# Odd mixer of a two-layer hybrid model: the first projection loaded as one block, smaller temporaries, and the mLSTM query and key products issued five chunks behind the convolution

## The chip, the core and the metric

The kernel runs on one core of one Trainium2 chip. The core has a matrix engine (TensorE, PE in the profile, with its weight loads as PEld), a vector engine (DVE), a scalar engine (ACT) and GpSimd (POOL), each with a queue of its own; SP issues most of the transfers from memory. The metric is the device time of one execution in microseconds; lower is better. Every time is that of the same inputs on the same kind of chip.

## The reference

The model has two layers on 256 rows of width 1024, all in float32. Each layer adds half a SwiGLU feed-forward block, then a mixer, then half of a second feed-forward block; the first layer's mixer is the even one (retention and gated linear attention), the second layer's the odd one (an RG-LRU and an mLSTM). The part that the change is about:

```python
def odd_mixer(hn, ...):
    ly, lx, mu, mv, mo, mi, mf = split_cols(hn @ w_in, ODD_SPLITS)
    lxc = causal_dwconv(f32(lx), f32(lru_conv_w), lru_conv_b)
    lru = rg_lru(lxc, ...)
    lru = lru * jax.nn.gelu(f32(ly))
    mc = jax.nn.silu(causal_dwconv(f32(mu), f32(ml_conv_w), ml_conv_b)).reshape(B, S, ML_HEADS, ML_DH)
    q = jnp.einsum('bshi,hij->bshj', mc, f32(ml_wq))
    k = jnp.einsum('bshi,hij->bshj', mc, f32(ml_wk)) * (ML_DH ** -0.5)
    hm = mlstm(q, k, f32(mv).reshape(B, S, ML_HEADS, ML_DH), f32(mi) + f32(ml_bi), f32(mf) + f32(ml_bf))
    hm = jax.nn.sigmoid(f32(mo)).reshape(B, S, ML_HEADS, ML_DH) * hm
    hm = head_rms(hm).reshape(B, S, -1) * f32(ml_norm_w)
    o = jnp.concatenate([lru, hm], axis=-1)
    return o.astype(hn.dtype) @ w_out
```

`hn @ w_in` is one product of 256 x 1024 with 1024 x 2568; `mi` and `mf` are the 8 gate columns at its end. The mLSTM weighs the products of q and k with a matrix E of exponentials that is made from the gates alone.

## The kernel before

**Precision and splits.** A float32 product is made of three faster ones. Each operand is split in two: `hi` is written by ACT (`split`, line 136) and `lo`, the rest, by DVE (line 137). `mm3` (line 215) then issues hi·hi (line 219), lo·hi (line 220) and hi·lo (line 222) for one block of 128 of the inner dimension; I call the three products of one block a chunk. Small products inside the mixers are plain float32.

**Rows.** The 256 rows are two halves of 128, t = 0 and t = 1. I write lx(0) for the unit lx with the first half. A normalized half stands transposed as `Th` (high) and `Tl` (low), made by `norm` (line 305): eight transposes on PE (line 318), eight `Th` on ACT (line 250), eight `Tl` on DVE (line 251).

**Units.** The program is a list of units, each with a `load` and a `run(t, w)`. The driver at the end of the kernel runs each unit for t = 0 as it comes, and for t = 1 some 1.5 units later (`LAG`). Around the odd mixer this gives the following order: the last blocks b8, b9, b10 of the feed-forward block's down projection (products into `acc`), then the mixer's six projections. mu0 makes 256 columns of mu and the 8 gate columns, mu1 the other 256 of mu, lx 512, mv 512, mo 512, ly 512. On PE this reads b10(0), b8(1), mu0(0), b9(1), mu1(0), b10(1), lx(0), mu0(1), mu1(1), mv(0), lx(1), mo(0) and so on. Four units of the output projection follow, and then the next feed-forward block.

**Rings.** `load_group` (line 139) takes a place in the ring `raw` (three places), has SP fill it, takes a place each in `hi` and `lo` (five places), and issues the splits. A place in `raw` is free again when its block is split, one in `hi` and `lo` when t = 1 has multiplied with it. A place is as large as the largest block of its ring: 2048 columns of float32 before. `proj_unit` (line 797) cuts a projection of n columns into groups of `g` blocks of the inner dimension: all 8 in one group for n up to 256, two groups of 4 above that. mu0 has n = 264 and so takes two groups of 4 x 264 = 1056 columns; mu1 takes one of 8 x 256 = 2048; lx, mv, mo and ly take two groups of 4 x 512 = 2048 each, which I call lx-a, lx-b, mv-a and so on. mu0's groups are split in steps of 2n = 528 columns, the others' in steps of 1024.

**Chains.** Work that hangs on a projection is a generator (`chain`, line 196), which yields a number of chunks after which its next part is issued (`STEPS`). `tick` counts the chunks that `mm3` has issued, those of 256 columns as half. `ml_chain` (line 1307) transposes mu, convolves it on DVE (twelve steps on line 1232), takes the silu by a tanh (line 1313 on ACT, line 1314 on DVE, which gives `mc`), yields `STEPS[18]`, then issues the query and key products (lines 1320 and 1321). `gate_chain` (line 1255) makes E from the gates with rows that are spread to all partitions through memory by POOL (`spread`). `lru_chain` does the same kind of work for lx.

**Order on an engine.** Each engine's instructions are put in order when the program is built: by the order in which they were issued, but with those that the builder expects to be ready placed ahead of those that it expects to wait. `issue_after` ties single ones.

**Temporaries.** Tiles of a mixer come from a pool; `mt(tag, shape, bufs)` says how many places a tag has. Places in question: `E3` and `gst` in the even mixer (lines 940 and 994), and in the odd mixer `mx` and `mrow` (lines 1273 and 1278) and `kw` (line 1336, the keys weighted with E, read on line 1353), and the results of `rsqrt_mean` (line 257). `mW` is the tag of a spread row (line 1287) that t = 1 needs.

Of the kernel before, what the change touches and what calls it, by code (L numbers as in the profile page):

```python
# [11 lines left out]
F32 = mybir.dt.float32  # L12
# [4 lines left out]
ALU = mybir.AluOpType  # L17
AX = mybir.AxisListType

P = 128  # L20
D = 1024
DFF = 2816
KC = D // P
# [23 lines left out]
TRP = 10  # L47
NT = 2
NTF = 10
STEPS = (2, 2, 10, 8, 3, 3, 6, 7, 3, 1, 1, 30, 10, 10, 9, 8, 3, 2, 10, 3, 3, 2, 9, 2, 3)  # L50

SUMS = (8, 4, 4)

# [15 lines left out]
def hybrid_kernel(ctx: ExitStack, tc: tile.TileContext, I, out):  # L69
    nc = tc.nc  # L70
    V, S, T, G = nc.vector, nc.scalar, nc.tensor, nc.gpsimd
# [3 lines left out]
    apool = ctx.enter_context(tc.tile_pool(name="act", bufs=1))  # L75
# [8 lines left out]
    def nm(s):  # L84
        cnt[0] += 1
        return f"{s}_{cnt[0]}"
# [4 lines left out]
    def mt(tag, shape, bufs=1, dt=F32):  # L91
        return pools[-1].tile(list(shape), dt, tag=tag, bufs=bufs, name=nm(tag))
# [161 lines left out]

    def rsqrt_mean(ss, n, w, name):
        m = apool.tile([P, w], F32, tag=f"rm{w}", bufs=2, name=nm("rm"))
        r = apool.tile([P, w], F32, tag=name, bufs=4, name=nm("rs"))
        G.tensor_scalar(out=m, in0=ss, scalar1=1.0 / n, scalar2=EPS, op0=ALU.mult, op1=ALU.add)
        G.tensor_tensor(out=r, in0=m, in1=mh4[:, :w], op=ALU.pow)
        return r  # L260
# [536 lines left out]
    def proj_unit(w_in, cols, body, mixer):  # L797

        wv = w_in.rearrange("(k p) n -> p k n", p=P)
        n = sum(w for _, w in cols)  # L800
        g = KC if n <= 256 else 4

        def load():
            return [load_group([wv[:, k0:k0 + g, c:c + w] for c, w in cols], g, n,
                               step=MSTEP[mixer] if n in (256, 512) else 2 * n) for k0 in range(0, KC, g)]

        def run(t, w):
            xT = get_x(t)
            ps = ps_tile()
            for k in range(KC):  # L810
                hi, lo = w[k // g]
                mm3([(ps[:, :n], slice(0, n))], xT, k, (hi[:, k % g, :], lo[:, k % g, :]), k == 0, k == KC - 1)
            body(t, ps[:, :n], state["rs"][t])
        return load, run, 0.5 if n < 300 else 1
# [57 lines left out]
    def even_units(w_in, w_lr_up, b_lr, w_out, nxt):  # L872
# [37 lines left out]
        def gla_chain(t, gl):  # L910
            d = st[t]
            yield STEPS[0]
            pt = ps_tile(tag="acc")
            T.transpose(pt[:16, :P], gl, ident)
            glT = mt("glTh", [16, P], 1, F32R), mt("glTl", [16, P], 1, F32R)
            split(pt[:16, :P], *glT)
            yield STEPS[1]
            pz = ps_tile(tag="acc")
# [6 lines left out]
            split(la, *lhl)  # L925
            yield STEPS[2]

# [9 lines left out]
                         start=True, stop=True)  # L937
            E1 = mt("E1", [P, 256])
            E2 = mt("E2", [P, 256])
            E3 = mt("E3", [P, 256], 2)  # L940
            E4 = mt("E4", [P, 256])
            dec = mt("dec", [P, 4], 2)
            S.activation(E1, pb[:, 256:], AF.Exp)
# [10 lines left out]
            V.scalar_tensor_tensor(out=E3, in0=k, scalar=0.125, in1=E3, op0=ALU.mult, op1=ALU.mult)  # L954
            yield STEPS[3]
            p1 = ps_tile(tag="acc")
# [14 lines left out]
            for p in range(2):  # L971
                for hh in range(2):
                    r = slice(hh * 64, hh * 64 + 64)
# [11 lines left out]
            for c in range(2 if t == 0 else 1):  # L985
                pu = ps_tile(tag="acc")
                r = slice(c * 64, c * 64 + 64)
# [3 lines left out]
                             v[r, hd, :], start=True, stop=True)  # L991
                upd.append(pu)
            for c, pu in enumerate(upd):
                sn = mt("gst", [P, 2, P], 3)
                if Sst[c] is None:
                    V.tensor_copy(f2(sn), pu[:, :256])
                else:
                    for p in range(2):
                        V.scalar_tensor_tensor(out=sn[:, p, :], in0=Sst[c][:, p, :],
                                               scalar=dec[:, 2 * p + c:2 * p + c + 1],  # L1000
                                               in1=pu[:, p * P:(p + 1) * P], op0=ALU.mult, op1=ALU.add)
                Sst[c + 1] = sn
# [14 lines left out]
            for p in range(2):  # L1017
                for hh, c in ((0, 0), (1, 1), (0, 1), (1, 0)):
                    if Sst[c] is None:
                        continue  # L1020
                    r, cc = slice(hh * 64, hh * 64 + 64), slice(c * 64, c * 64 + 64)
# [138 lines left out]
    def odd_units(w_in, prm, w_out, nxt):  # L1160
# [94 lines left out]
        def gate_chain(t, g8):  # L1255
            d = st[t]
            lf = mt("lf", [P, 4])
            logsigmoid(lf, g8[:, 4:8], "f", 4)
            yield STEPS[14]
            pb = ps_tile(tag="acc")  # L1260
            T.matmul(pb[:, 0:4], C["tri"], lf, start=True, stop=True)
            ab = mt("ab", [P, 2, 4], 2)
            V.tensor_copy(ab[:, 1, :], pb[:, 0:4])
            V.tensor_tensor(out=ab[:, 0, :], in0=g8[:, 0:4], in1=ab[:, 1, :], op=ALU.subtract)
            yield STEPS[15]
            pr = ps_tile(tag="acc")
            T.transpose(pr[:4, 0:P], ab[:, 0, :], ident)
            T.transpose(pr[:4, P:2 * P], ab[:, 1, :], ident)
            arow = mt("arow", [4, 2 * P])
            S.copy(arow, pr[:4, 0:2 * P])  # L1270
            if t == 1:
                yield lambda: "m1" in C
            mx = mt("mx", [4, P], 2)
            V.tensor_tensor_scan(out=mx, data0=arow[:, 0:P], data1=arow[:, 0:P],
                                 initial=0.0 if t == 0 else C["m1"], op0=ALU.max, op1=ALU.max)
            rows = {}
            spread(rows, "E", mx, "mE", 3)
            mrow = mt("mrow", [4, P])
            V.tensor_tensor(out=mrow, in0=arow[:, P:2 * P], in1=mx, op=ALU.add)
            if t == 0:  # L1280
                m1 = mt("m1", [4, 1])
                V.tensor_copy(m1, mrow[:, P - 1:P])
                C["m1"] = m1
            else:
                wi = mt("wi", [4, P])
                S.activation(wi, mx, AF.Exp, scale=-1.0, bias=C["m1"])
                spread(d, "wi", wi, "mW", 3)
            yield STEPS[16]
            pq = ps_tile(tag="acc")
            T.transpose(pq[:, 0:4], mrow, ident[:4, :4])  # L1290
            guard = mt("guard", [P, 4], 2)
            S.activation(guard, pq[:, 0:4], AF.Exp, scale=-1.0)
            yield lambda: "E" in rows
            yield STEPS[24]
            E = rows["E"]
            for hd in range(4):
                V.scalar_tensor_tensor(out=E[:, hd, :], in0=E[:, hd, :], scalar=ab[:, 0, hd:hd + 1],
                                       in1=C["big"], op0=ALU.subtract, op1=ALU.max)
            S.activation(f2(E), f2(E), AF.Exp, scale=-1.0)
            d["E"], d["guard"] = E, guard  # L1300
# [6 lines left out]
        def ml_chain(t, u):  # L1307
# [25 lines left out]
            V.tensor_tensor(out=f2(Sw), in0=psS, in1=f2(E), op=ALU.mult)  # L1333
            if t == 0:
                pk2 = transposes(f2(kT), 4)
                kw = mt("mkw", [P, 4, P])
                for hd in range(4):
                    V.tensor_scalar(out=kw[:, hd, :], in0=pk2[:, hd * P:(hd + 1) * P], scalar1=E[:, hd, P - 1:P],
                                    scalar2=None, op0=ALU.mult)
            else:  # L1340

                yield has(t, "wi")
                V.tensor_tensor(out=f2(qT), in0=f2(qT), in1=f2(d["wi"]), op=ALU.mult)
# [18 lines left out]
            for p in range(2):  # L1362
                pn = ps_tile(tag="acc")
                last = None
                for i in range(2):
                    hd = 2 * p + i
                    sl = slice(i * (P + 1), (i + 1) * (P + 1))
                    with after(last):
                        last = T.matmul(pn[:, sl], Sw[:, hd, :], v[:, hd, :], start=True, stop=t == 0)
                        if t == 1:  # L1370
# [8 lines left out]
                                in1=den[:, hs].unsqueeze(2).to_broadcast([P, 2, P]), op=ALU.mult)  # L1379
# [225 lines left out]
```

## Time and profile before

| | us |
|---|---|
| median of 3 runs | 953.7 |
| lowest and highest run | 952.96, 953.75 |
| the profiled execution | 954.01 |
| its span, first to last instruction | 952.2 |
| PE busy in the span | 941.4 |
| DVE busy | 826.4 |
| ACT busy | 616.1 |
| weight loads busy (PEld) | 777.2 |

A row of the timeline gives the start in microseconds, the length, the engine, the line of the kernel, the operation, what is written and what is read, the shape, and how many equal instructions were merged; in square brackets stands the idle time of the engine just before and what ended it. A number after `x` in a group is the count of instructions, and the next the mean or the range of their durations in ns. Ends of PE's products are modelled: the records of two products that follow each other overlap, so PE's speed is read from the distance of starts. The odd mixer's projections and chains run from about 660 to 760 us.

### The profile page before, as it was taken

What the parts mean: (1) busy time and instruction counts of PE and PEld (TensorE: products, weight loads), DVE (VectorE), ACT (ScalarE), POOL (GpSimd) and SP (SyncE); (2) the same over time, 40 slices, a digit from 0 to 9 for tenths busy, and PEclk for the clock granted to TensorE, in tenths of its full rate; (3) what the DMA queues carried; (4) which work ended last, traced back from release to release, by engine and by line L of the source; (5) the groups of instructions that cost most, each with busy time, mean ns of one, the idle gap of its engine ahead of it and who ended that gap; (6) DMA issues with size and microseconds to landing.
All of it is one profiled execution on the core that took longest, in us unless ns stands there. A gap on an engine that the chain in (4) does not pass through costs nothing.

```text
span 952.2 us, 11885 instructions
## 1 busy us (share of the span) xinstructions
PE 941.4 (99%) x4526; PEld 777.2 (82%) x4526; DVE 826.4 (87%) x970; ACT 616.1 (65%) x815; POOL 22.6 (2%) x49
## 2 busy tenths in 40 slices
PE   9999999999999999999999999999999999999997
PEld 6888888888888888888888888888888788888876
DVE  6999999687776999998489999955797999999996
ACT  7647567584656665765476656654899767566564
POOL 1000000000100000000000000000101000000000
PEclk9999999999999999999999999999999999999999
DMA  9876463755358555649461935474452782944521
GB/s 304 281 279 209 146 221 98 220 172 198 100 185 281 208 183 215 237 138 334 145 229 45 322 108 188 143 229 154 136 183 72 252 321 68 329 151 160 177 89 66
DMA packets 103529, 180.32 MB, mean 189 GB/s; under 512 B 8277, under 2 KB 51441, under 8 KB 103473
## 3 DMA queue, kind: packets, MB, share of 16 engines
q1 hardware_dynamic: 102704, 178.23, 55.5%
q0 software_dynamic: 336, 0.79, 0.3%
q8 instruction: 35, 0.57, 0.2%
q10 hardware_dynamic: 432, 0.55, 0.2%
q14 instruction: 22, 0.17, 0.1%
HBM read 178.50 MB, written 1.05 MB: 189 GB/s over the span
## 4 chain that ended last, share of the span: by engine, by line
PE 84%; DVE 10%; issue 2%; ACT 2%; DMA 1%; POOL 0%; POOLq 0%; ACTq 0%; DVEq 0%
PE ps L653 21%; PE ps L219 11%; PE ps L220 11%; PE ps L222 11%; PE acc L220 8%; PE acc L219 8%; PE acc L222 8%; DVE lo L137 5%; DVE draw L670 2%; PE ps L680 1%; ACT hi L136 1%; PE ps L236 1%; DMA h<-in_x_dram 0%; DVE cs L670 0%; DMA draw<-in_ffn_wgu_dram 0%
## 5 line engine op out<-in xcount | busy, mean ns | idle before, releaser
L137 DVE TENSOR_TENSOR lo<-raw,hi 128x512 fp32r<-128x512 f32 (+4 forms) x211 | 289.9, 1398 | 41.5 <-ACT hi L136 41.4
L136 ACT ACTIVATE hi<-raw 128x512 fp32r<-128x512 f32 (+4 forms) x211 | 244.2, 1197 | 50.6 <-PE ps L222 21.8
L219 PE MATMUL ps<-hi,Th 128*128 128x512 f32 (+3 forms) x512 | 199.2, 389 | 0.3 <-ACT Th L250 0.2
L220 PE MATMUL ps<-lo,Th 128*128 128x512 f32 (+3 forms) x512 | 193.8, 379 | 1.0 <-DVE lo L137 1.0
L222 PE MATMUL ps<-hi,Tl 128*128 128x512 f32 (+3 forms) x512 | 193.8, 379 | 0.0
L137 DVE TENSOR_TENSOR lo<-draw,hi 128x2048 fp32r<-128x2048 f32 (+1 forms) x86 | 182.4, 2138 | 10.0 <-ACT hi L136 10.0
L136 ACT ACTIVATE hi<-draw 128x2048 fp32r<-128x2048 f32 (+1 forms) x86 | 153.8, 1799 | 50.5 <-DVE draw L670 38.1
L219 PE MATMUL acc<-hi,aT 128*128 128x512 f32 x350 | 137.7, 396 | 1.2 <-ACT hi L136 1.2
L220 PE MATMUL acc<-lo,aT 128*128 128x512 f32 x350 | 135.8, 390 | 0.0
L220 PEld LDWEIGHTS ps<-lo,Th 128*128 128x128 f32 x512 | 96.5, 188 | 18.4 <-DVE lo L137 2.4
L219 PEld LDWEIGHTS ps<-hi,Th 128*128 128x128 f32 x512 | 96.2, 188 | 18.0 <-issue 0.7
L222 PE MATMUL acc<-hi,aT 128*128 128x512 f32 x350 | 110.8, 390 | 0.0
L222 PEld LDWEIGHTS ps<-hi,Tl 128*128 128x128 f32 x512 | 96.2, 188 | 17.8 <-DVE Tl L137 0.2
L670 DVE TENSOR_TENSOR draw<-draw,draw 128x2048 f32<-128x2048 f32 x39 | 89.1, 2287 | 2.8 <-DVE lo L137 1.8
L136 ACT ACTIVATE aT<-ps 128x256 fp32r<-128x256 f32 x88 | 33.3, 379 | 77.2 <-PE ps L236 43.9
L219 PEld LDWEIGHTS acc<-hi,aT 128*128 128x128 f32 x350 | 65.7, 188 | 14.7 <-ACT hi L136 1.6
L222 PEld LDWEIGHTS acc<-hi,aT 128*128 128x128 f32 x350 | 65.7, 188 | 13.9
L220 PEld LDWEIGHTS acc<-lo,aT 128*128 128x128 f32 x350 | 65.6, 188 | 12.8 <-DVE lo L137 0.2
L653 PE MATMUL ps<-hi,Th 128*128 128x512 f32 x156 | 61.2, 392 | 0.0
L653 PE MATMUL ps<-hi,Tl 128*128 128x512 f32 x156 | 60.8, 390 | 0.0
L653 PE MATMUL ps<-lo,Th 128*128 128x512 f32 x156 | 60.8, 389 | 0.0
L137 DVE TENSOR_TENSOR aT<-ps,aT 128x256 fp32r<-128x256 f32 x88 | 36.9, 421 | 11.7 <-ACT aT L136 11.3
(379 smaller groups left out, 1279.0 us busy)
## 6 DMA issues: line engine op xcount, KB each, us to landing
raw<-in_ffn_wd_dram SPq DMA_DIRECT2D x44, 1024.0 KB, 5.3
draw<-in_ffn_wgu_dram SPq DMA_DIRECT2D x39, 1024.0 KB, 6.6
raw<-in_ffn_wgu_dram SPq DMA_DIRECT2D x64, 512.0 KB, 5.0
raw<-in_ffn_wgu_dram SPq DMA_DIRECT2D x13, 1024.0 KB, 6.3
raw<-in_e_w_in_dram SPq DMA_DIRECT2D x13, 1024.0 KB, 5.1
raw<-in_o_w_in_dram SPq DMA_DIRECT2D x9, 1024.0 KB, 5.2
raw<-in_e_w_out_dram SPq DMA_DIRECT2D x4, 1024.0 KB, 4.9
raw<-in_o_w_out_dram SPq DMA_DIRECT2D x4, 1024.0 KB, 4.9
```

The costliest lines, as they stand in the source:

```text
L136: S.activation(hi2, src2, AF.Copy)
L137: V.tensor_tensor(out=lo2, in0=src2, in1=hi2.bitcast(F32), op=ALU.subtract)
L219: T.matmul(ps, xh[:, k, :], wk[0][:, sl], start=start, stop=False)
L220: T.matmul(ps, xh[:, k, :], wk[1][:, sl], start=False, stop=False)
L222: state["mm"] = T.matmul(ps, xl[:, k, :], wk[0][:, sl], start=False, stop=stop)
L236: T.transpose(pt[:, i * P:(i + 1) * P], src[:, i * P:(i + 1) * P], ident)
L653: state["mm"] = T.matmul(ps, x[a][:, k, :], w[b][:, k, :], start=first and k == 0 and i == 0, stop=k == 3 and i == 2, skip_group_check=not ...
L670: state["dve"] = V.tensor_tensor(out=out, in0=a, in1=b, op=op)
L680: T.transpose(pt[:, i * P:(i + 1) * P], a[:, i * P:(i + 1) * P], ident)
```

## The change

1. `proj_unit` puts all 8 blocks into one group for n up to 264, so that mu0 becomes one load of 8 x 264 = 2112 columns in place of two of 1056. Its split keeps steps of 528 columns. The places of all three rings, thirteen in all, grow from 2048 to 2112 columns, 256 bytes per partition each.
2. Temporaries get fewer places: `E3` one instead of two, `gst` two instead of three, `mx` one instead of two, the four-wide results of `rsqrt_mean` two instead of four; `mrow` is computed in place in the second half of `arow`; `kw` shares the one place of `mW`.
3. `STEPS[18]` is 5 instead of 10: the query and key products are issued five chunks after the convolution.

```diff
-STEPS = (2, 2, 10, 8, 3, 3, 6, 7, 3, 1, 1, 30, 10, 10, 9, 8, 3, 2, 10, 3, 3, 2, 9, 2, 3)
+STEPS = (2, 2, 10, 8, 3, 3, 6, 7, 3, 1, 1, 30, 10, 10, 9, 8, 3, 2, 5, 3, 3, 2, 9, 2, 3)
...
-        r = apool.tile([P, w], F32, tag=name, bufs=4, name=nm("rs"))
+        r = apool.tile([P, w], F32, tag=name, bufs=4 if w == 1 else 2, name=nm("rs"))
...
-        g = KC if n <= 256 else 4
+        g = KC if n <= 264 else 4
...
-            E3 = mt("E3", [P, 256], 2)
+            E3 = mt("E3", [P, 256])
...
-                sn = mt("gst", [P, 2, P], 3)
+                sn = mt("gst", [P, 2, P], 2)
...
-            mx = mt("mx", [4, P], 2)
+            mx = mt("mx", [4, P])
...
-            mrow = mt("mrow", [4, P])
-            V.tensor_tensor(out=mrow, in0=arow[:, P:2 * P], in1=mx, op=ALU.add)
+            mrow = arow[:, P:2 * P]
+            V.tensor_tensor(out=mrow, in0=mrow, in1=mx, op=ALU.add)
...
-                kw = mt("mkw", [P, 4, P])
+                kw = mt("mW", [P, 4, P], 1)
```

## The prediction, made before the changed kernel was timed

> **What bounds the kernel now.** I read the page first, then the busy times by stretch, the waits of PE in the odd mixer, and the timeline around the longest of them.
>
> ```profile
> span 952.2 us, 11885 instructions
> ...
> PE 941.4 (99%) x4526; PEld 777.2 (82%) x4526; DVE 826.4 (87%) x970; ACT 616.1 (65%) x815; POOL 22.6 (2%) x49
> ```
>
> ```profile
> 660.00:674.50 14.50, 14.50 (x94) 12.89 (x93) 8.64 (x20) 10.91 (x20) 2.03 (x3) 1.00 0.24 76
> 674.50:683.00 8.50, 7.34 (x37) 5.72 (x36) 8.40 (x21) 7.41 (x15) 0.00 (x0) 1.00 0.43 127
> ...
> 692.50:722.00 29.50, 29.09 (x169) 24.29 (x169) 28.28 (x79) 26.61 (x48) 2.29 (x5) 1.00 0.45 152
> ...
> 940.00:952.20 12.20, 6.03 (x33) 5.05 (x31) 7.10 (x18) 4.84 (x17) 0.00 (x0) 0.87 0.26 93
> ```
>
> The columns of the second view are the stretch, its length, the busy time of PE, PEld, DVE, ACT and POOL, the granted clock and the DMA. PE is idle for 952.2 − 941.4 = 10.8 us in all, of which 6.2 lie in the last stretch, behind the last product. No edit here removes a product, so a gain can only be PE time that is lost to waits. In the mixer the largest such place is 674.5 to 683.0: PE is idle for 1.16 us, and DVE is busy for 8.40 of 8.50 us. For those 8.5 us DVE is the bound. In the 14.5 us before it DVE works only 8.64.
>
> ```profile
> PE ps L220 <- DVE lo L137: 1.0, 1, 1.0
> ```
>
> This is the longest of PE's waits from 625 to 760 us. A PE record is longer than its issue distance, so a wait is partly hidden in it; I measure by the distance of starts instead.
>
> ```profile
> 662.52 0.28 PE L219 MATMUL ps<-hi,Th 128*128 128x264 f32 x1
> ...
> 665.30 0.28 PE L222 MATMUL ps<-hi,Tl 128*128 128x264 f32 x1
> ...
> 668.19 0.28 PE L219 MATMUL ps<-hi,Th 128*128 128x256 f32 x1
> ...
> 674.50 0.39 PE L219 MATMUL ps<-hi,Th 128*128 128x512 f32 x1
> 674.73 0.39 PE L220 MATMUL ps<-lo,Th 128*128 128x512 f32 x1
> ...
> 677.43 0.39 PE L219 MATMUL ps<-hi,Th 128*128 128x512 f32 x1
> ...
> 678.46 0.27 PE L1268 MATMUL acc<-ident,ab 128*4 128x128 f32 x1
> 678.93 0.39 PE L219 MATMUL ps<-hi,Th 128*128 128x264 f32 x1 [0.19 <-ACT Th L250]
> 679.15 0.28 PE L220 MATMUL ps<-lo,Th 128*128 128x264 f32 x1
> 680.40 0.50 PE L220 MATMUL ps<-lo,Th 128*128 128x512 f32 x1 [0.96 <-DVE lo L137]
> 680.74 0.40 PE L222 MATMUL ps<-hi,Tl 128*128 128x512 f32 x1
> ...
> 683.03 0.38 PE L1320 MATMUL acc<-mc,wqk 128*128 128x128 f32 x2
> ```
>
> lx(0), the unit lx for the first 128 rows, starts at 674.50. Products of 512 columns start 0.23 us apart; the 24 of mu0(0), 264 columns each, start from 662.52 to 665.30, 2.78 / 23 = 0.12 apart. From 679.15 to 680.74 there are 1.59 us where a 264 and a 512 need 0.12 + 0.23 = 0.35: 1.24 lost. From 678.46 to 679.15 there are 0.69 where a transpose and a 264 after it need at most 0.34 as an estimate (0.12 for each and 0.10 for the change of shape): 0.35 lost. Together **1.6 us**. The product that waits is the second block of lx, of which the low half is not split yet.
>
> ```profile
> 671.20 2.36 DVE L137 TENSOR_TENSOR lo<-raw,hi 128x1024 fp32r<-128x1024 f32 x2 [0.79 <-ACT hi L136]
> ...
> 675.60 3.61 DVE L1232 SCALAR_TENSOR_TENSOR mc<-mlcb,mlcw,mc 128x128 f32<-128x128 f32 x12
> 679.12 2.36 DVE L137 TENSOR_TENSOR lo<-raw,hi 128x1024 fp32r<-128x1024 f32 x2
> 681.39 0.35 DVE L251 SCALAR_TENSOR_TENSOR Tl<-ps,nw,Th 128x128 fp32r<-128x128 f32 x1
> 681.65 0.69 DVE L1314 SCALAR_TENSOR_TENSOR mc<-mE,mc 128x512 f32<-128x512 f32 x1
> ...
> 684.47 0.34 DVE L251 SCALAR_TENSOR_TENSOR Tl<-acc,nw,Th 128x128 fp32r<-128x128 f32 x1
> ```
>
> ```profile
> 661.02 0.37 ACT L250 ACTIVATE Th<-ps,nw 128x128 fp32r<-128x128 f32 x1 [3.00 <-PE ps L318]
> ...
> 676.62 2.00 ACT L136 ACTIVATE hi<-raw 128x1024 fp32r<-128x1024 f32 x2
> ...
> 679.65 1.28 ACT L1313 ACT_TABLE_LOAD   x1
> 680.95 0.64 ACT L1313 ACTIVATE mE<-mc 128x512 f32<-128x512 f32 x1
> ```
>
> The split of that block (ACT 676.62, DVE 679.12) comes behind the twelve steps of the mLSTM convolution on DVE. It could not start before 674.5: hi and lo are rings of five, and five loads ahead of it stands the last block of the FFN's down projection, whose products for the second 128 rows run until lx(0) starts.
>
> **The change part by part.**
>
> *One block for the first projection (term A).* The mixer's loads before are mu0a, mu0b, mu1, lx-a, lx-b, mv-a and so on; after, mu0 is one. Every load from mu1 on takes the ring place that its predecessor had: lx-a waits for the third-last block of the down projection, whose last user ends where mu0(0) begins (662.5), instead of the second-last (668.19, where mu1(0) begins); lx-b for the second-last, instead of the last (674.5). mv-a takes over the wait for the last. So lx-a's split can move to where mu1's stands now, and lx-b's to where lx-a's stands now (ACT about 670, DVE 671.20 to 673.56), over 4 us ahead of its first use, which is after four of lx's chunks and eight transposes. The cover is DVE's 14.50 − 8.64 = 5.9 us of idle time from 660 on; mu1's split moves in front, where ACT idles 3.00 us before 661.02. The same number of products, splits (4 x 528 columns for mu0 in both) and bytes stays; SP issues two transfers instead of four, and nothing waits for SP here. Term A: **−1.6 us**, between 0 and −1.6.
>
> *Query and key products five chunks behind (term D).* They are sixteen fp32 matmul records of the wqk lines, first at 683.03, right behind lx(0): ten chunks after the convolution was issued, two of them in the last down projection, eight in lx(0). Five chunks put them into the order behind lx's third chunk, before 677.43. They need mc, which now comes at 681.65 + 0.69 = 682.3. The convolution ends at 675.60 + 3.61 = 679.2; then tanh (0.64) and L1314 (0.69) make 680.5 where the table load (1.28) lies under the convolution, and 681.8 where it does not. With term A lx(0) ends at 683.03 − 1.6 = 681.4. Whether the built order lets the products wait for mc or fills in others is seen at the second half:
>
> ```profile
> 705.77 0.39 PE L220 MATMUL ps<-lo,Th 128*128 128x512 f32 x1
> 706.15 0.46 PE L1320 MATMUL acc<-mc,wqk 128*128 128x128 f32 x2
> ```
>
> ```profile
> 705.31 0.69 DVE L1314 SCALAR_TENSOR_TENSOR mc<-mE,mc 128x512 f32<-128x512 f32 x1 [0.33 <-ACT mE L1313]
> ```
>
> There the ten chunks are long over (mv(0) and lx(1) were being multiplied), and the products stand in the middle of a chunk at 706.15, where mc was ready at 706.00. The order was made by when operands come, and it was right to 0.15 us (706.15 − 705.77 = 0.38 against 0.23). The wait at 680.40 shows that it can be 1.2 us wrong. Bounds of D: 0 to +1.2; I take **+0.4**, which is 681.8 − 681.4. Earlier products feed nothing that is late: what follows them waits for E, which is made from the gates.
>
> *The smaller temporaries (cost 0).* Each now shares a buffer whose last reader is long done:
>
> ```profile
> 209.23 0.97 PE L990 MATMUL acc<-gv,E 64*64 64x128 f32 x16
> ...
> 214.07 0.65 PE L1023 MATMUL acc<-gst,gqiT 64*64 64x128 f32 x8
> ```
>
> ```profile
> 221.72 0.40 ACT L946 ACTIVATE E<-acc 128x256 f32<-128x256 f32 x1
> ```
>
> ```profile
> 233.94 0.60 DVE L999 SCALAR_TENSOR_TENSOR gst<-gst,dec,acc 128x128 f32<-128x128 f32 x2
> ```
>
> ```profile
> 708.01 1.06 PE L1353 MATMUL acc<-v,mkw 128*128 128x129 f32 x8
> ```
>
> ```profile
> L1251 POOL DMA_DIRECT2D mW<-r x1: 553/553/553, 720.3 to 720.3; - x1
> ```
>
> E3 is read until 210.2 and written again at 221.72; the first gst is read until 214.7 and its place written at 233.94; kw is read until 709.1 and the broadcast into its place starts at 720.3. These leave 11, 19 and 11 us. mx, the row that now holds mrow and the rsqrt tiles are written once for each half, and between the two writes stand whole projection units. If one of these covers went, the wait would fall on ACT, DVE or POOL, not on PE directly.
>
> **Sum.** −1.6 + 0.4 = −1.2 us. The profiled execution took 954.01, 1.8 more than its span; the median of the runs is 953.7. From the execution: 952.8; from the median: **952.5**.
>
> **The rivals.**
>
> *The wait changes hands (same).* mv-a's split (2.36 on DVE, 2.00 on ACT) can now start at 674.5 and might take the place of lx-b's. Then the low halves of the second norm still run from 681.39 to 684.81, while PE, 1.6 us earlier, wants mu0(1). Its chunks take 3 x 0.12; the last would start near 681.4 + 7 x 0.36 = 683.9 and wait 0.9 us: net −1.6 + 0.9 + 0.4 = −0.3, **953.4**. For it: DVE has no idle time there. Against: mv is issued after mu1(1), behind the norm, so where both are ready the norm goes first. Here also belongs that nothing moves: 953.7.
>
> *The products come too early (slower).* If they stay behind lx's third chunk, PE stops at 677.43 until mc comes, at 681.3 (without lx-b's split ahead) to 682.3. That is 3.9 to 4.9 us, which cover the lost 1.6: net +2.3 to +3.3, **956.0 to 957.0**. It decides from 1.6 us of waiting on. Against it stands the place at 706.15; for it, that PE did stand still behind one L220 at 679.15. The Trainium skill, "TensorE: Matmul & The Clock Gate", Step-by-step: what each phase is for, says that matmuls keep the program's order and only weight loads are pulled ahead; by that rule nothing behind these products could fill such a wait, and the trace agrees at 679.15. The same page, Part 1: The HAM clock gate, says that an idle stretch of about 3.4 us halves the clock until PE has worked as long again; by it a wait of 4.9 us could cost an estimated 1.7 us more, 958.7; the trace shows a granted clock under 1.00 only in the last stretch above (0.87), where PE is half idle.
>
> *More goes than the one wait (faster).*
>
> ```profile
> 719.27 0.39 PE L222 MATMUL ps<-hi,Tl 128*128 128x512 f32 x1
> 720.07 2.05 PE L1415 MATMUL acc<-xc,wax 128*128 128x128 f32 x16 [0.41 <-DVE xc L1232]
> ```
>
> DVE is busy for 28.28 of 29.50 us up to 722, and its 2.36 us less of work left over could also end this wait: 0.80 where 0.23 is needed, 0.57 lost. With D at 0 that makes −1.6 − 0.57 = −2.2, **951.5**. Against: PE also arrives 1.6 us earlier.
>
> **How the numbers follow.** My forecast (a gain of 0.6 to 1.8 us, 951.9 to 953.1) gets 0.50, the wait that changes hands 0.20, more than the one wait 0.18, products too early 0.12. About 0.2% (1.9 us) is what a measurement of this kernel can tell from no change. Faster needs under 951.8: nearly all of the 0.18 and a little of the forecast's edge, 0.19; slower needs over 955.6: 0.12; the rest, 0.69, is the same. The range goes from 951.3 (951.5 with a little spread) to 954.7, which takes in the wait that changes hands and a D of 1.2 with it (−1.6 + 0.9 + 1.2 = +0.5, 954.2) with the spread of the runs; it leaves out the slower rival.
>
> **What would show it.** Right: no wait of PE for lo of lx near 679; lx-b's low half on DVE before the convolution of mc; mu0(1) ends about 1.2 us earlier; the stretch from lx(0)'s start to the first wqk product shorter than 8.5 us. Wrong: a wait of PE for mc at L1320 over 1.6 us; a wait for Tl or Th of the second norm of 1 us; a new wait in the even mixer for E3 or gst; or the same products after 722 us with more idle time than before, which would give the gain back.

## The result and the profile after

The changed kernel takes **963.59 us** (median of four runs, 962.63 to 964.55), the kernel before in the same session 953.37 (952.96 to 953.75). The ratio is 1.0105, with a 95% interval from 1.0094 to 1.0117: 10.2 us slower, where 952.5 with a range of 951.3 to 954.7 was predicted. The profiled execution took 964.44. Executions that were disturbed (two of the four of the first experiment) are left out of the times and ratios given here.

The page of the changed kernel: PE does the same 4526 products and is counted busy 6.3 us longer (941.4 before), in a span that is 10.5 us longer.

```profile
span 962.7 us, 11884 instructions
...
PE 947.7 (98%) x4526; PEld 778.6 (81%) x4526; DVE 828.4 (86%) x970; ACT 619.6 (64%) x817; POOL 24.1 (2%) x49
```

Busy times by stretch, in the changed kernel (columns as in the prediction: stretch, length, PE, PEld, DVE, ACT, POOL, granted clock, DMA):

```profile
674.50:683.00 8.50, 8.50 (x46) 7.15 (x45) 8.37 (x24) 5.89 (x13) 0.00 (x0) 1.00 0.41 138
...
692.50:722.00 29.50, 26.83 (x153) 23.11 (x152) 23.50 (x63) 25.00 (x43) 0.69 (x2) 0.94 0.34 111
...
700.00:702.00 2.00, 0.31 (x2) 0.31 (x3) 2.00 (x4) 1.97 (x3) 0.00 (x0) 1.00 0.00 0
702.00:704.00 2.00, 2.00 (x11) 1.74 (x10) 1.34 (x5) 1.97 (x4) 0.00 (x0) 0.65 0.79 214
704.00:706.00 2.00, 2.00 (x7) 1.68 (x6) 1.51 (x4) 2.00 (x8) 0.00 (x0) 0.50 0.83 318
```

The wait that the prediction was about is gone: PE is busy for all of 674.5 to 683. The price comes later. Between 692.5 and 722 DVE, which was busy for 28.28 us before, now has 6 us to spare, and PE loses 2.67. A stall up to 701.7 is followed by 3 to 4 us at a granted clock of 0.65 and 0.50, which before stayed at 1.00.

PE's waits from 640 to 780 us, and the products around the first two of the places where it loses time:

```profile
PE acc L1415 <- DVE mSw L1333: 2.7, 1, 2.7
PE ps L220 <- DVE lo L137: 2.1, 2, 1.4
PE acc L1320 <- issue: 0.8, 1, 0.8
...
```

```profile
677.19 0.40 PE L219 MATMUL ps<-hi,Th 128*128 128x512 f32 x1
...
683.54 0.28 PE L219 MATMUL ps<-hi,Th 128*128 128x264 f32 x1
...
684.02 0.28 PE L220 MATMUL ps<-lo,Th 128*128 128x264 f32 x1
685.10 0.46 PE L1320 MATMUL acc<-mc,wqk 128*128 128x128 f32 x2 [0.79 <-issue]
...
698.62 0.40 PE L222 MATMUL ps<-hi,Tl 128*128 128x512 f32 x1
701.69 1.26 PE L1415 MATMUL acc<-xc,wax 128*128 128x128 f32 x8 [2.67 <-DVE mSw L1333]
```

lx(0) starts at 677.19 instead of 674.50. So **2.7 us are lost before lx(0) begins**, where PE waits no longer than before. From there to the first query and key product it is 7.91 us, 0.62 less than the 8.53 of before. lx(0) itself now runs without a wait, from 677.19 to 683.54; behind it five products of 264 columns need 0.60 us, and 0.96 of the 1.56 us up to 685.10 are lost waiting. Then comes the stall of 701.69: the second half of the recurrent unit's gate products (line 1415) needs one of the four `acc` banks, and these are held by products that wait for E. DVE's timeline leads there:

```profile
673.90 2.36 DVE L137 TENSOR_TENSOR lo<-raw,hi 128x1024 fp32r<-128x1024 f32 x2 [0.79 <-ACT hi L136]
...
678.29 3.61 DVE L1232 SCALAR_TENSOR_TENSOR mc<-mlcb,mlcw,mc 128x128 f32<-128x128 f32 x12
...
691.85 2.97 DVE L1232 SCALAR_TENSOR_TENSOR xc<-lrucb,lrucw,xc 128x128 f32<-128x128 f32 x11
697.55 1.14 DVE L1297 SCALAR_TENSOR_TENSOR mE<-mE,ab,big 128x128 f32<-128x128 f32 x4 [2.73 <-DMA mE<-r]
698.61 0.15 DVE L849 SCALAR_TENSOR_TENSOR fe<-g 128x4 f32<-128x4 f32 x1
698.68 2.35 DVE L137 TENSOR_TENSOR lo<-raw,hi 128x1024 fp32r<-128x1024 f32 x2
700.95 0.68 DVE L1333 TENSOR_TENSOR mSw<-acc,mE 128x512 f32<-128x512 f32 x1
```

lx-b's low half now stands ahead of the convolution (673.90 against 678.29), as predicted. But at 694.8 DVE reaches the instruction that makes E and stands for 2.73 us, since the row that POOL spreads through memory has not landed. Queued behind it are the next split and the product with the scores (`mSw`) that would free a bank. In the kernel before, mv-a's split (2.36 us at 687.78) stood between the second norm and the convolution of xc, and DVE reached E at 693.21 without a wait; now that split is done by 687.2, in two parts at 682.85 and 685.95. DVE in the kernel before:

```profile
687.78 2.36 DVE L137 TENSOR_TENSOR lo<-raw,hi 128x1024 fp32r<-128x1024 f32 x2
690.06 3.24 DVE L1232 SCALAR_TENSOR_TENSOR xc<-lrucb,lrucw,xc 128x128 f32<-128x128 f32 x12
693.21 1.13 DVE L1297 SCALAR_TENSOR_TENSOR mE<-mE,ab,big 128x128 f32<-128x128 f32 x4
```

### The profile page after: what moved, and what is told of

It is laid out like the page before. It is cut to its first block, busy times and chain, and to the rows that moved or that the text cites. A ratio compares the mean times of both kernels' runs of the same rounds, so it can differ in the third digit from the quotient of the medians.

```text
span 962.7 us, 11884 instructions
## 1 busy us (share of the span) xinstructions
PE 947.7 (98%) x4526; PEld 778.6 (81%) x4526; DVE 828.4 (86%) x970; ACT 619.6 (64%) x817; POOL 24.1 (2%) x49
## 4 chain that ended last, share of the span: by engine, by line
PE 92%; DVE 3%; DMA 2%; ACT 1%; issue 1%; POOL 0%; POOLq 0%; SPq 0%; DVEq 0%; ACTq 0%
PE ps L653 26%; PE ps L219 11%; PE ps L220 11%; PE ps L222 11%; PE acc L219 9%; PE acc L222 9%; PE acc L220 9%; PE ps L680 1%; DMA raw<-in_ffn_wgu_dram 1%; DVE lo L137 1%; PE ps L236 1%; DMA r<-mx 0%; DMA wB<-in_final_norm_dram 0%; DMA mE<-r 0%; DVE lh L1438 0%
```

## The experiments

I write "aligned" for the changed kernel with two temporaries cut to one place, which puts the mixer's pools back to their old place modulo 256 bytes.

**Undo one part at a time.** First the changed kernel with the old ten chunks, and the kernel before with the new five.

```diff
-STEPS = (2, 2, 10, 8, 3, 3, 6, 7, 3, 1, 1, 30, 10, 10, 9, 8, 3, 2, 5, 3, 3, 2, 9, 2, 3)
+STEPS = (2, 2, 10, 8, 3, 3, 6, 7, 3, 1, 1, 30, 10, 10, 9, 8, 3, 2, 10, 3, 3, 2, 9, 2, 3)
```

> The changed kernel with the query and key products ten chunks behind again (STEPS[18] = 10); one block and small temporaries stay. Theory A (two causes: the five chunks put the products of wqk ahead of the two transposes of the gate rows, L1267 and L1268, which then wait for an acc bank, E comes late and PE stands; and the tiles behind the rings begin 64 bytes further in their 256, which makes each product with an S tile 6.5 ns longer, 624 of them, 4.1 us): the mixer's loss goes, the 4.1 us stay, so 953.4 - 1.3 + 4.1 = 956 us, no wait of PE over 1 us between 660 and 770 us, L1267 before L1320. Rival B (the one block in the ring upsets the order by itself): 961 to 964 us, and the wait at L1415 stays.

Measured: 965.36 and 966.38, ratio 1.0128 [1.0108, 1.0148], above both ranges; no trace of these two executions exists.

> The kernel before with five chunks alone (STEPS[18] = 5), rings and temporaries as before. Theory A: L1267 and L1268 come behind the products of wqk, E is late, PE waits about 3 us at L1415 and the rest of the mixer loses as in the changed kernel: 957 to 960 us. Rival B (the five chunks do harm only with the one block): 953 to 954 us.

Measured: 954.03, ratio 1.0005 [0.9995, 1.0014]. The five chunks alone cost nothing that can be told, and without them the one block is no better (about 2 us worse). The products' distance, the one thing that the prediction had feared, is not by itself the cause. In the trace of this run the gates' rows are transposed at 684.01, behind the query and key products as in the changed kernel, and DVE still meets E without a wait.

**The time lost before the mixer.** On PE the order of the products is the same in both kernels up to there, yet the distance grows steadily. It grows at the products of line 653, the feed-forward block's, whose stationary tiles are `S1h` to `S4l`. The group of one such tile, in the profile of before and of after (count: shortest, median, longest record in ns, first and last start, shape):

```profile
L653 PE MATMUL ps<-hi,S2h x52: 389/389/389, 74.7 to 914.7; 128*128 128x512 f32 x52
```

```profile
L653 PE MATMUL ps<-hi,S2h x52: 393/398/398, 74.3 to 925.0; 128*128 128x512 f32 x52
```

From start to start, 616 pairs of products on these tiles take 227.0 ns before and 233.3 after; the same line with `Th` and `Tl` keeps its 389 ns records. What differs is only where the tiles lie. The larger rings (13 places of 256 bytes more) and smaller rsqrt tiles (192 bytes less) move the pools behind them by 3136 bytes, which is 64 more than a multiple of 256: by the compiled placement the S tiles start 224 bytes past a multiple of 256 instead of 160, while hi, lo, Th and Tl stay at 160. Two runs move that place and nothing else; the order of instructions on each engine is that of the kernel they start from.

```diff
-            state["ms"][t] = (apool.tile([P, 2], F32, tag="ms", bufs=2, name=nm("ms")),
+            state["ms"][t] = (apool.tile([P, 2], F32, tag="ms", bufs=4, name=nm("ms")),
```

> The kernel before with two more 32-byte places of the tag ms, the last but one of its pool: every tile of the later pools begins 64 bytes higher (S1h at 224 instead of 160 in its 256), with the same instructions in the same order on every engine. Theory A: distance of two products with an S tile 233 instead of 227 ns, 953.4 + 4.1 = 957.5 us. Rival C (the longer distance is a state of the run, or comes from the rings' own new places): 953.4 us and 227 ns.

Measured: 957.51 (957.36 to 957.69), ratio 1.0040 [1.0025, 1.0055], as the theory had it.

```diff
-        m = apool.tile([P, w], F32, tag=f"rm{w}", bufs=2, name=nm("rm"))
-        r = apool.tile([P, w], F32, tag=name, bufs=4 if w == 1 else 2, name=nm("rs"))
+        m = apool.tile([P, w], F32, tag=f"rm{w}", bufs=2 if w == 1 else 1, name=nm("rm"))
+        r = apool.tile([P, w], F32, tag=name, bufs=4 if w == 1 else 1 if name == "r4m" else 2, name=nm("rs"))
```

> The changed kernel with two places of 32 bytes fewer (rm of width 4 and r4m one place each): S1h begins at 160 in its 256 again, the rings stay at 2112, and every engine has the instructions in the same order. Theory A: 227 ns, 963.6 - 4.1 = 959.5 us, the waits of the mixer as they are. Rival C: 963.6 us and 233 ns.

Measured: 959.54 (957.95 to 960.6), ratio 1.0057 [1.0041, 1.0074]. Both ways it is 4 us, and 624 products times 6.3 ns make 3.9. Of these, 432 lie ahead of lx(0): 2.7 us, what lx(0) is late by.

Whether it is the place itself or the distance between a product's two operands, a map by itself tells.

> The whole computation is left out: it loads x and writes it back, and between them multiplies: 64 bursts of 16 products (128x128 by 128x512, the block products' type), each pair of a stationary tile at 128, 160, 192, 224, 0, 32, 64 or 96 bytes past a multiple of 256 with a moving tile at one of these; then the same 64 bursts with VectorE and ScalarE reading and writing SBUF beside them. Theory (the weights' address modulo 256 sets the distance of starts): near 227 ns at 160 and 232.5 or more at 224, with DVE and ACT idle too, the moving address without effect. Rival (it is a conflict with what other engines read and write): 227 everywhere in the first 64 bursts, and a difference only in the second. Rival (what counts is the distance of the weights' address from the moving operand's): the pairs with equal distance agree, not those with equal weights.

Part of PE's timeline there; bursts of 16 products with the moving tile `mD` at 224 and the stationary tiles `wB` at 160, `wC` at 192, `wD` at 224, `wE` at 0 and `wF` at 32:

```profile
101.31 3.84 PE L48 MATMUL ps<-mD,wB 128*128 128x512 f32 x16
105.00 3.89 PE L48 MATMUL ps<-mD,wC 128*128 128x512 f32 x16
108.72 3.80 PE L48 MATMUL ps<-mD,wD 128*128 128x512 f32 x16
112.36 3.89 PE L48 MATMUL ps<-mD,wE 128*128 128x512 f32 x16
116.08 3.90 PE L48 MATMUL ps<-mD,wF 128*128 128x512 f32 x16
```

The burst with both at 224 takes 3.64 us, or 227 ns each; `wE`, `wF` and `wC` take 3.72, or 232. All eight diagonals of the map are alike, with DVE and ACT idle or busy: by the stationary address less the moving one, modulo 256, the distance of starts (the mean of a burst, and of these the middle value) is 226.7 ns at 0 (228.4 to 228.8 for the pairs of the two lowest tiles, and the first burst of all left out), 233.0 at 32, 233.5 at 64, 233.7 at 96, 232.4 at 128, 233.3 at 160, 229.5 at 192 and 233.3 at 224. So the second rival was right and my theory wrong: not the place counts but the distance. In the kernel: 224 less 160 is 64, 233.5 in the map and 233.3 in the trace. The last test moves both operands together.

```diff
-    mh4 = cpool.tile([P, 4], F32, tag="mh4", name="mh4")
+    mh4 = cpool.tile([P, 20], F32, tag="mh4", name="mh4")
```

> The kernel before with 64 bytes more in front of the rings, so that hi, lo, Th, Tl, aT and S1h to S4l all move together from 160 to 224 past a multiple of 256. Theory (what counts is the distance between a product's two operands modulo 256 bytes, 0 before): 953.4, same as before, distance of starts 227 ns on line 653. Rival (the place 224 itself is slow for the stationary tiles): 957.5 or more, since now Th, Tl and aT stand there too.

Measured: 954.01, ratio 1.0005 [0.9995, 1.0014], and the tile's group is back at 389:

```profile
L653 PE MATMUL ps<-hi,S2h x52: 389/389/389, 74.2 to 914.7; 128*128 128x512 f32 x52
```

**The rest, about 6 us, in the mixer.** The one block with ten chunks, aligned:

> The changed kernel with its query and key products ten chunks behind as before, and with the two one-place rsqrt tiles, so that the products' stationary tiles stand where they stood before. Theory (the one block itself moves the mixer's order, whatever the products' distance): the time stays above before by 4 us or more, 957.5 to 962.5. Rival (only the two edits together harm: the products five chunks behind push the gates' rows back): with the products late again the loss goes and the one block's gain shows, 952 to 954.

Measured: 961.52, ratio 1.0085 [1.0068, 1.0102]. The one block does the harm without the five chunks. (The smaller temporaries are still in; no run tries the one block without them.) From the timeline of this run, DVE, ACT and PE:

```profile
693.83 1.14 DVE L1297 SCALAR_TENSOR_TENSOR mE<-mE,ab,big 128x128 f32<-128x128 f32 x4 [3.03 <-DMA mE<-r]
```

```profile
695.05 0.63 ACT L1299 ACTIVATE mE<-mE 128x512 f32<-128x512 f32 x1 [4.50 <-DVE mE L1297]
695.59 0.46 ACT L1241 ACTIVATE cu<-ps,rs 128x256 f32<-128x256 f32 x1
```

```profile
692.81 0.39 PE L222 MATMUL ps<-hi,Tl 128*128 128x512 f32 x1
696.10 0.80 PE L868 MATMUL acc<-ident,cu 128*128 128x128 f32 x4 [2.90 <-ACT cu L1241]
```

DVE stands 3.03 us for the spread row, ACT 4.50 behind DVE, and in ACT's queue behind that stands the copy of `cu` that PE needs: PE stops for 2.90. Here it is not a bank, but it is E again.

Three theories of the mixer's loss were then tried: banks, the place of the gates' rows, and the trip through memory.

```diff
-                pg = ps_tile(tag="acc")
+                pg = ps_tile()
```

> The aligned changed kernel (959.5), with the recurrent unit's gate products (acc<-xc,wax, line 1415) put into the ps banks, which the block products use, instead of the acc banks. Theory (PE stands for 2.8 us before the second gate product because the four acc banks are held by products that wait for the late E, and the clock halves behind it): both go, 955 to 956.5. Rival (PE runs out of other work there, whichever bank the gates use: then something else waits as long): 958.5 to 960.

Measured: 958.75 (957.32 to 960.79), ratio 1.0059 [1.0042, 1.0076], in the rival's range. The stall moves on: PE waits 1.9 us at the gates' sums of the second half (line 1261), and the lo waits behind stay.

```diff
-            pr = ps_tile(tag="acc")
+            pr = ps_tile()
```

> The aligned changed kernel (959.5), with the two transposes of the gates' rows (acc<-ident,ab, line 1268) put into a ps bank instead of an acc bank. Theory (these rows stand behind the query and key products for want of an acc bank, and that makes E late): they start before 682, the broadcast mE comes 4 us or more earlier, the wait before the second gate product is under 1 us, and the time is 954 to 956. Rival (E is late because its broadcast lands late behind the 1 MB load issued at the same time, and the rows' place matters little): the rows come early but E by under 2 us, 957.5 to 960.

Measured: 956.31, ratio 1.0032 [1.002, 1.0044], 0.3 us above the theory's range. The gates' rows are transposed at 678.1 instead of 683.8, as they were before, and the time falls by 3.2 us; but the broadcast of mE is issued only 1.2 us earlier (689.65 against 690.86). The theory had said 4 and missed that: the trip of the row to memory takes 4.82 us here. Next the trip itself was replaced, first in this kernel, then in the kernel before.

```diff
-            r = dpool.tile([4, P], F32, tag="r", bufs=2, name=nm("r"))
-            G.dma_start(r, row)
...
-                G.dma_start(all_, r.unsqueeze(0).to_broadcast([P, 4, P]))
...
-            defer(n, back)
+                pb = ps_tile()
+                for hd in range(4):
+                    T.matmul(pb[:, hd * P:(hd + 1) * P], ident[:4, hd:hd + 1].to_broadcast([4, P]), row, start=True, stop=True)
...
+                S.copy(f2(all_), pb)
...
+            defer(1, back)
```

> The aligned changed kernel with the gates' rows in a ps bank (956.3), and the gates' rows mx and wi are spread over the partitions by four products with a column of the identity each, instead of by a DMA to HBM and one back. Theory (after the banks, what is left of the loss is E, which lands late because both transfers stand behind a 1 MB load: DVE waits 1.5 us for it, and PE 1.5 and 1.8 us at the gate products): DVE waits for no DMA of mE, and the time is 952.5 to 954.5, the products themselves costing 0.9 us for each of three spreads where nothing hides them. Rival (the trip is hidden, and the rest of the loss is in other waits): 956.3 to 959.

Measured: 955.66 (954.58 to 956.93), ratio 1.0023 [1.0013, 1.0032]: PE's stalls at the gate products are gone, but in the profiled execution the granted clock is 0.77 and 0.50 from 686 to 690, which loses 1.5 us, and the spreads' own products come on top; the time is 1.2 us above my range.

> Control: the kernel before, with the same spread by products and nothing else. In its own profile DVE never waits for mE (it has the splits of the two half blocks to do meanwhile). Theory (there the trip was hidden): no gain, 953.4 to 956, the products' cost. Rival (the trip's latency was on the path before too): 950 to 952.5.

Measured: 960.55, ratio 1.0072 [1.0057, 1.0087], above both ranges. The busy times by stretch of this run:

```profile
715.00:720.00 5.00, 3.63 (x15) 3.04 (x16) 4.73 (x16) 4.23 (x9) 0.00 (x0) 0.73 0.04 15
720.00:730.00 10.00, 10.00 (x41) 8.21 (x40) 6.41 (x15) 4.13 (x7) 0.00 (x0) 0.79 0.32 107
```

PE idles for 1.37 us of the first stretch, and the clock loses 5 x 0.27 + 10 x 0.21 = 3.5 us. It was not followed further: the edit adds products on PE and copies on ACT as well as making the chain shorter, and which of these costs the 7 us is open.

**Why the trip is long.** SP's load and POOL's transfers in the changed kernel, then in the kernel before:

```profile
687.23 0.37 SPq L151 DMA_DIRECT2D raw<-in_o_w_in_dram  x1
```

```profile
689.00 0.75 POOL L1247 DMA_DIRECT2D r<-mx  x1 [0.81 <-DVE arow L1279]
694.10 0.58 POOL L1251 DMA_DIRECT2D mE<-r  x1 [4.35 <-DMA r<-mx]
```

```profile
685.44 0.75 POOL L1247 DMA_DIRECT2D r<-mx  x1 [18.91 <-DVE mlcb L1223]
...
688.70 0.65 POOL L1251 DMA_DIRECT2D mE<-r  x1 [1.27 <-DMA r<-mx]
```

From the row's issue to the spread's it is 5.10 us after and 3.26 before. Before, the last load had been issued at 681.51, 3.9 us ahead of the row; the next, which waits for mv-a's split to free its place in `raw`, at 690.17, behind it. After, mv-a's split is early, and this load leaves 1.8 us ahead of the row. The traces of the other kernels go the same way. With the load 3.9 us ahead the trip takes 2.88 to 3.26 us (the kernel before and its three variants with that lead), with 5.1 us it takes 2.05 (five chunks alone). With 1.77 us it takes 4.98 to 5.10 (the changed kernel, aligned, and with E later), with 0.95 us 4.63 to 4.82 (five kernels). One does not fit: with the gates in ps it took 3.84 at 1.77. A first probe of this was of no use, since the builder moved the transfers out of their rounds:

> The whole computation is left out: it loads x and writes it back. Between them, sixteen times, POOL sends a 4x128 row to HBM and, when it has landed, spreads it back over 128 partitions, as the gates' rows are; in all but four of them SP issues a 1 MB load of weights (128x2048) 0 to some 5 us ahead. Theory (a small transfer issued close behind the load waits for it): from the row's issue to the spread's issue 3 us or less without a load, 4.5 to 5 with the load 1 to 2 us ahead, and back to 3 where the load is 4 us or more ahead. Rival (the load does not matter, the long trips had another cause): the same time in all sixteen.

Measured: the first rows were issued ahead of the first load, so nothing can be read from it. The second chains them:

> The whole computation is left out: it loads x and writes it back. Between them, sixteen times one after the other, POOL sends a 4x128 row to HBM and, when it has landed, spreads it back over 128 partitions, as the gates' rows are; in twelve of them SP issues a 1 MB load (128x2048) at the start and POOL fills 0 to 7 times 0.52 us before it issues the row. Theory (a small transfer issued close behind the load waits for it): from the row's issue to the spread's 3 us or less without a load, 4.5 to 5 with the load 1 to 2 us ahead, back to 3 where it is 4 us or more ahead. Rival (the load does not matter): the same in all sixteen.

POOL's timeline, the loads 1.0, 1.6, 2.8 and 4.0 us ahead of these rows:

```profile
17.58 0.54 POOL L51 DMA_DIRECT2D r<-row  x1 [0.29 <-POOL row L48]
22.35 0.57 POOL L52 DMA_DIRECT2D mE<-r  x1 [4.24 <-DMA r<-row]
...
31.71 0.54 POOL L51 DMA_DIRECT2D r<-row  x1 [0.29 <-POOL row L48]
35.83 0.57 POOL L52 DMA_DIRECT2D mE<-r  x1 [3.58 <-DMA r<-row]
...
60.71 0.54 POOL L51 DMA_DIRECT2D r<-row  x1 [0.29 <-POOL row L48]
63.58 0.57 POOL L52 DMA_DIRECT2D mE<-r  x1 [2.33 <-DMA r<-row]
...
75.34 0.54 POOL L51 DMA_DIRECT2D r<-row  x1 [0.29 <-POOL row L48]
77.64 0.56 POOL L52 DMA_DIRECT2D mE<-r  x1 [1.76 <-DMA r<-row]
```

4.77, 4.12, 2.87 and 2.30 us; in the second eight rounds 4.96, 4.20, 2.93 and 2.30. Without a load the four trips took 3.41, 2.92, 1.89 and 2.28. So a row issued 1 us behind the load waits for it, and at 4 us it does not. At 1.6 us the probe lies under the 4.5 that the theory gave, and about 1 us under what the kernels show at 1.77; that difference is not explained. (The Trainium skill, "DMA: Bandwidth & Descriptors", section "Latency and other measured facts", gives memory an access latency of 0.2 us on average and 2 us at high load; the 2.5 to 2.7 us between the longest and the shortest of these trips are of that size, but no run here tells such a latency from a wait in a queue.)

**Put E behind the splits.** If the harm is that DVE and ACT stand at E with the next splits and copies queued behind, it should go when E's steps are issued later, and nothing else is touched. The same last number was set in three kernels; the diff is that of the first, against the one block with ten chunks, aligned.

```diff
-STEPS = (2, 2, 10, 8, 3, 3, 6, 7, 3, 1, 1, 30, 10, 10, 9, 8, 3, 2, 10, 3, 3, 2, 9, 2, 3)
+STEPS = (2, 2, 10, 8, 3, 3, 6, 7, 3, 1, 1, 30, 10, 10, 9, 8, 3, 2, 10, 3, 3, 2, 9, 2, 10)
```

> The one block with the products ten chunks behind, aligned (961.5), and E's steps on DVE and ACT issued ten chunks behind the row's broadcast instead of three, so that the mv and mo splits and the copies of cu stand ahead of them. Theory (DVE stands 3.0 us for E's transfer and ACT 4.5 us behind it, with the copy of cu and the next splits queued behind; that is what PE's 3 us and part of the later waits come from): the 3.05 us at L868 go, and the time is 955 to 958. Rival (PE runs out of work there for another reason): 960 to 963.

Measured: 954.73, ratio 1.0021 [1.0011, 1.003]; 6.8 us less than the same kernel without this edit, and slightly under the theory's range.

> The aligned changed kernel with the gates' rows in a ps bank (956.3), and E's steps ten chunks behind instead of three, as in the run above. Theory: DVE's 1.5 us wait for E goes, but the scores stay longer in their acc bank and the second gate product waits for it; where the splits were the larger part 953.5 to 955.5. Rival (the bank is the larger part): 957 to 959.

Measured: 954.48, ratio 1.0012 [1.0002, 1.0022]; 1.8 us less than without this edit.

> The aligned changed kernel (959.5) with E's steps ten chunks behind its broadcast instead of three, and nothing else. Theory (DVE and ACT standing for E in front of the splits is most of the 6 us): 954 to 956. Rival (with the products five chunks behind, the missing acc bank holds PE as long whatever DVE and ACT do, and a later E makes it worse): 959 to 961.

Measured: 955.12, ratio 1.0021 [1.0011, 1.003]: 4.4 us less by that one number, in the changed kernel itself. Its DVE timeline and its stretch of the mixer:

```profile
691.41 2.36 DVE L137 TENSOR_TENSOR lo<-raw,hi 128x1024 fp32r<-128x1024 f32 x2
693.68 0.69 DVE L1224 COPY mlcb<-acc 128x512 f32<-128x512 f32 x1
694.28 0.35 DVE L1297 SCALAR_TENSOR_TENSOR mE<-mE,ab,big 128x128 f32<-128x128 f32 x1
```

```profile
692.50:722.00 29.50, 27.86 (x159) 23.51 (x157) 26.24 (x68) 27.13 (x47) 2.27 (x5) 1.00 0.47 161
```

The row's trip is as long as without the edit (4.98 us against 5.02), and E is made at the same time (694.28 against 694.27), but nobody stands for it: the splits come first, PE is busy 27.86 us instead of the 26.46 of the aligned changed kernel, and the clock stays at 1.00 instead of 0.94, which is 29.5 x 0.06 = 1.8 us more. Two last runs, one to look for a gain, one as control:

> The one block, aligned, E's steps ten chunks behind (954.7), and the query and key products thirteen chunks behind instead of ten. With ten, PE still loses 0.47 and 0.61 us before these products, for mc. Theory (they are too early by that much): both go, 953.2 to 954.2. Rival (later products make the scores, and what waits for them, late): 955 to 957.

Measured: 956.99, ratio 1.0037 [1.0023, 1.0051], in the rival's range.

> Control: the kernel before with E's steps ten chunks behind instead of three. Theory (DVE did not wait for E there, so nothing is to be had): 953 to 955, not faster. Rival (E's place is worth something by itself, whatever the blocks): 950 to 952.5.

Measured: 953.15, ratio 0.9997 [0.9988, 1.0007]. Where DVE did not stand for E, the number does nothing. No version came out faster than the kernel before.

## Why the prediction was wrong

The 10.2 us, by differences of medians (the kernel before had 953.2 to 953.6 in the other sessions): 963.59 − 959.54 = **4.05 from the address**, 959.54 − 955.12 = **4.42 from DVE and ACT standing at E**, and 955.12 − 953.37 = 1.75 that stay. The ratios of the aligned kernel and of the one with E later are known to 1.6 and 0.9 us either way, so the last two shares are rough; the first has the 3.9 of the test in the kernel before beside it. The second includes what the clock loses behind the stall.

- **Term A, −1.6.** Right in its mechanism: the place in the rings, lx-b's split ahead of the convolution, no wait of PE for lo near 679. lx(0) takes 6.35 us from start to end, which is the 8.53 of before less the 1.6 lost and about 0.6 for the two products of 264 columns and the two transposes that stood inside it. To the first wqk product 0.62 us of the 1.6 are left, since term D's wait lies in between. The step that failed is its cover: "DVE's 14.50 − 8.64 = 5.9 us of idle time" was taken as room for work that moves ahead, and what DVE and ACT do with the time that becomes free was not asked. That work had filled the time in which E is on its way. Without it they reach E's instructions early, in an order fixed when the program is built, and stand in front of the splits that PE needs.
- **Term D, +0.4, bounds 0 to +1.2.** PE stands 0.79 us for mc (line 1320), 0.96 by starts, inside the bounds and over the +0.4. But "Earlier products feed nothing that is late: what follows them waits for E, which is made from the gates" failed, though only together with the one block. The products took the banks that the gates' rows needed, and these were pushed behind them (from 678.35 to 686.96); giving the rows another bank takes 3.2 us off. The push alone does no harm: with five chunks in the kernel before the rows come at 684.01, the trip takes 2.05 us and the time is that of before. Nor is it needed: with ten chunks and the one block the rows come at 678.67, and DVE stands 3.03 us for E all the same. And E had at most about 1 us of slack before: DVE came to it at 693.21, the spread was issued at 688.70, and from the spread's issue to the end of DVE's wait it is 3.4 to 3.6 us in the kernels in which DVE waits, 4.4 with the gates in ps.
- **"SP issues two transfers instead of four, and nothing waits for SP here".** Nothing waited for SP, but POOL's small transfer did wait behind what SP had issued: 5.10 us instead of 3.26.
- **The smaller temporaries, cost 0.** No wait of PE came for any of them. What was missing is the line before it: the rings' growth was stated as 256 bytes per place and never priced. It moved the S tiles by 64 bytes modulo 256 against the other operand of 624 products, for 4 us, more than the whole gain that was in sight.
- **The rivals.** "The products come too early" was right in its sign and wrong in its place: PE did not stop at 677 but at 698.6, for E. The clock did fall as that rival's note said it could: two stretches of 2 us at 0.65 and 0.50 with PE busy all through lose 2 x 0.35 + 2 x 0.50 = 1.7 us. In the aligned changed kernel the two longer executions (960.21 and 960.60) have a mean granted clock of 0.996 and the two shorter ones (958.88 and 957.95) of 0.998 and 0.999, which fits a clock that falls in some executions and not in others; that was not tested by itself. The Trainium skill, "TensorE: Matmul & The Clock Gate", Part 1: The HAM clock gate, ties the fall to a window of about 3.4 us that runs free of the program; here it followed a gap of 3.07 us between starts (698.62 to 701.69), and did not follow one of 3.29 (692.81 to 696.10) in the one block with ten chunks. So a bound on the length of a wait is not safe from either side.

What stays open: the 1.75 us. With E behind the splits PE's waits from 640 to 780 us are 4.2 us in all, against 1.8 before: 0.8 before the first wqk product, 1.4 before the second half's gate sums (line 1261) and 1.2 for a low half are the largest. Thirteen chunks instead of ten, in the one block with E later, did not help, and no run splits that remainder.

## What to carry to other kernels

An edit that resizes a ring moves every tile behind it: compare the places of both operands of the most frequent products modulo 256 bytes before any timing, and put back what moved. Work that is moved ahead on an in-order engine leaves a hole where it stood; look for the instruction that now comes first in that hole and waits for a transfer, and issue it behind the work that others need. An idle share of an engine is not slack if its next instruction stands in front of a long trip through memory.

## What the runs showed of the hardware

- The distance of two 128x128 by 128x512 products is 227 ns (229 for two of the eight pairs tried) where both operands start at the same place modulo 256 bytes, 229.5 where the stationary one starts 64 bytes lower, and 232.4 to 233.7 at the other distances tried (multiples of 32), with DVE and ACT idle or busy.
- A 2 KB transfer to memory takes 1.9 to 3.4 us until the next step by itself in the probe, 4.8 to 5.0 when a 1 MB load was issued 1 us ahead, and 2.3 when 4 us ahead. In the kernels it takes 4.6 to 5.1 us with a load 0.95 or 1.77 us ahead (3.84 once), 2.9 to 3.3 with one 3.9 us ahead and 2.05 with one 5.1 us ahead.
- The granted clock fell to a half after a gap of 3.07 us between products, and stayed at 1.00 after one of 3.29 in another kernel. It also fell, to 0.50 from 688 to 690 us, in the kernel with the rows in ps and no trip, where the longest distance of starts nearby is 1.56 us (680.46 to 682.02).
